# Dead products in the first stage's waits, two page gathers issued elsewhere, and strided copies turned round, in a TensorE-bound decoder layer

## Chip, cores and metric

One core of one Trainium2 chip. The metric is the device time of one execution in microseconds, as a median over runs. Lower is better.

## What is computed

One layer of a hybrid decoder over 512 prompt tokens and 32 sample tokens (8 sequences of 4), width 1024, all float32: a modulated RMS norm, then two mixers fed by one projection (sparse attention with a compressed, a selected and a window branch; a convolution module), merged by gates, one output projection, and a SwiGLU FFN of width 2816 with norms round it. Cut to what the change touches:

```python
ada = silu(c) @ w_ada + b_ada                     # six parts: shift, scale, gate, twice
h = rms_norm(x, g[0]) * (1 + sc_m) + sh_m
q, kv, g, glu, mg = split(h @ w_in)               # 16 heads, 4 kv heads, head width 64
conv_in = a * sigmoid(b)                          # a, b = split(glu), 512 channels
o_conv = silu(layer_norm(depthwise_conv31(hist))) @ w_pw2
# past keys and values: cache_kv[page_table], 4 pages of 128 rows for each of 8 sequences
k_c = gelu(flat(blocks of 32 rows) @ w_cmp1 + b_cmp1) @ w_cmp2     # and v_c
y = (ga * (gates of o_cmp, o_slc, o_win) + gb * o_conv) @ w_out
```

## The kernel before

**Products.** Nearly all the work is TensorE's. A float32 weight tile (`wraw`, 128 x 1024) is split into a high part (`wh`, ACT, L168) and a low part (`wl`, DVE, L171), the activations likewise (`hh`, `hl`). A half tile is 8 + 8 + 8 products of 128 x 272 (`hh·wh`, `hl·wh`, `hh·wl`), a tile two halves for the 544 tokens. All products but transposes go through one helper line, L165.

**Order.** Python code emits the program by events at hand-written times: `ev(t, f)` calls `f` at planner time `t`, `spawn` steps a generator whose `yield`s are times, `when(kind, n)` is the time of a weight. The weights come in the order of a plan, through rings of a few raw buffers (`wraw`, `araw`, `xraw`) loaded by SP's queue; a load starts when the buffer's last reader is done. A scheduler then orders each engine's rows by that order and by what it thinks is ready. Each engine works strictly in its order.

**First stage (0 to 69 us).** `x` is loaded, squared and summed; 18 + 21 `warm` products of a constant tile (`mm(dst, wt, src)`, result never read) run beside that. `rstd_from` turns the sums (products of 1 column). `conditioning(h)` makes half of the modulation vectors: eight `ada_product`s of raw weights with `cs` (32 columns, 256 wide), then `ada_quarters` (an eviction to `adaz`), `ada_first` (two transposes) and DVE work that ends with `A0`. `rows(k)` norms one of 8 row blocks, `opened(k)` makes the first three projection tiles (`w0h`, `w0l`) on it: blocks 0 to 3 after conditioning(0), 4 to 7 after conditioning(1).

**Pages.** The sample group's past comes as 32 pages, in four gathers `load_pages(bq)` of 8 indirect DMAs each on POOL's queue (L431). Gathers 0 and 2 share one buffer, 1 and 3 another, which later holds `Xc`. `paced(0, A0[:, 7, 8:9])` makes gather 0 wait, on POOL, for a one-element copy of `A0` of conditioning(1). `compress_pages(bq, kd)` are 16 products `pv<-X,w1t`, called pv(bq, kd) here.

**Convolution.** For each of four channel blocks POOL multiplies the sample windows (`cpr`, L638), DVE reduces them (L639), then 31 taps run on DVE, with the `wl` splits between. `compress_prompt` copies the prompt's keys and values (`zt`) into `Xc` on ACT (L762); near it ACT also evicts `K` (L719), and `qz` (L842), which `pt<-selq,qz` on TensorE needs.

**Attention and FFN.** Groups g = 0 to 3 with units i = 0 to 3: scores, exponentials `PB` on ACT, scaling on POOL and DVE, transposes (`big<-c,PB`, L1073) and value products, with the weight half tiles between. Then output projection, second norm and FFN.

Of the kernel before, what the change touches and what calls it, by code (L numbers as in the profile page):

```python
# [35 lines left out]
TP = 512  # L36
# [29 lines left out]
NF = 12  # L66
# [13 lines left out]
def _plan():  # L80

    p = [(0.1 * n, "ada", n) for n in range(8)] + [(1 + 0.1 * n, "glu", n) for n in range(NG)]
    p += [(2.345 + 0.1 * n, "ada", n) for n in range(8, 16)]
    p += [(43.845 + 6.5 * (n - NG), "glu", n) for n in range(NG, 8)]
    p += [(76.23 + 10.0 * n, "kv", n) for n in range(12)]
    p += [(60.955 + 5.024 * n, "ada", 16 + n) for n in range(16)]
    p += [(at(3, 1.759 + 0.428 * n), "ada", 32 + n) for n in range(16)]
    p += [(164, "g", 0)]
    p += [(205.59 + 3.412 * n, "pw2", n) for n in range(8)]
    p += [(111.427 + 9.999 * n, "qs", n) for n in range(8)]  # L90
    p += [(TA + 6.4 * n, "q", n) for n in range(2)]
    for g in range(4):
        if g < 3:
            p += [(at(g, 6.173 if g == 0 else 5.336), "q", 2 * g + 2), (at(g, 9.865) - 1.608, "q", 2 * g + 3)]
        p += [(at(g, 12.127 + 0.25 * n) if g < 3 else at(3, 0.321 + 0.9 * n), "ga", 2 * g + n) for n in range(2)]
# [17 lines left out]
def body(ctx, tc, xT, cT, cst, sel, vecs, b1row, wall, w1, pool_rows, kwin, vwin, convst, ptab,  # L113
# [356 lines left out]
    with tc.tile_pool(name="p0", bufs=1) as p0:  # L470
# [40 lines left out]
        def conditioning(h):  # L511
            p = P_pt()
            for k in range(8):
                raw, tag = take("ada", 8 * h + k)
                ada_product(p, k, raw)
                raw_done(tag)
            ada_first(h, ada_quarters(p))
            r = slice(4 * h, 4 * h + 4)
            first.append(dve.scalar_tensor_tensor(A0[:, r], adaT[:, 1, r], 1.0, gains[:, 0, r, None].to_broadcast([128, 4, 9]),
                                     op0=OP.add, op1=OP.mult))  # L520
# [109 lines left out]
    def conv(ct, t, step):  # L630

        y = cy[:, ct, :TP]
        ys = cy[:, ct, TP:].rearrange("p (b t) -> p b t", t=4)
        b = vc[:, V_BDW + ct:V_BDW + ct + 1]
        hs0 = hst[:, ct, :, 0:4]
        win = bass.AP(tensor=hs0.tensor, offset=hs0.offset, ap=[hs0.ap[0], [34, 8], [1, 4], [1, 31]])
        pr_ = cp.tile([128, 8, 4, 31], F32, name="cpr", tag="cpr", bufs=1)
        pool.tensor_mul(pr_, win, dw[:, ct, None, None, :].to_broadcast([128, 8, 4, 31]))  # L638
        dve.tensor_reduce(ys, pr_, axis=AX.X, op=OP.add)  # L639
        dve.tensor_scalar(ys, ys, b, None, op0=OP.add)  # L640
        for k in range(31):
            yield t + step * k
            w = dw[:, ct, k:k + 1]
            if k == 0:
                dve.tensor_scalar(y, hist[:, ct, 0:TP], w, b, op0=OP.mult, op1=OP.add)
            else:
                dve.scalar_tensor_tensor(y, hist[:, ct, k:k + TP], w, y, op0=OP.mult, op1=OP.add)  # L647

    def layer_norm(t):
# [99 lines left out]
    def compress_prompt(t):  # L749
        yield t - 12  # L750
        Xc = xp.tile([128, 2, 16, 64], F32, name="Xc", tag="X1")
# [3 lines left out]
        for kd in range(2):  # L755
            for pr in range(2):
                for h2 in range(2):
                    g = 2 * pr + h2
                    src = zts[kd, pr][64 * h2:64 * h2 + 64, 0:TP].rearrange("p (b l r) -> p r l b", b=16, r=2)
                    for r in range(2):  # L760
                        o = Xc[64 * r:64 * r + 64, kd, :, g * 16:g * 16 + 16]
                        act.activation(o, src[:, r], AF.Copy)  # L762
# [66 lines left out]
    def q_sample(f):  # L829
# [60 lines left out]
    spawn(99.808, compress_prompt(142.311))  # L890
    ada_b2 = []
# [127 lines left out]
    def unit(g, i, t, dq, dp):  # L1019
# [79 lines left out]
    def attn(g):  # L1099
        ev(at(g, 0) + 0.005, split_keys, g)  # L1100
        spawn(at(g, 0.15), compressed(g, at(g, 0.15)))
# [6 lines left out]

        ev(at(g, 0) + 6.411, units)

    def sample_attn(t0, step):
# [46 lines left out]
        yield t0 + 7.845  # L1158
        p = P_sc()
# [12 lines left out]
        for b in range(8):  # L1172
# [169 lines left out]
    def second_norm(hf, t, step):  # L1342
# [428 lines left out]
```

## Time and profile before

| | us |
|---|---|
| median of 3 runs (lowest to highest) | 1059.93 (1059.86 to 1061.65) |
| profiled execution | 1055.7 |
| its span in the trace | 1053.9 |
| TensorE busy | 1015.5 |

The profiled execution is 0.4% below the median, so a sum worked out from the trace is scaled by 1059.93/1055.7 before it is set against the median. The page's rows give for each group of instructions its busy time, and then the idle time of its engine just ahead of it with what ended that. TensorE's clock is given as a share of full speed: at 1.00 a 128 x 272 product takes 0.125 us of its queue, at 0.5 about 0.23.

### The profile page before, as it was taken

Reading aid. Unit: us, or ns where it says so; the run is one execution under the profiler, and the core shown is the slowest. Engines: PE = TensorE matmul, PEld = TensorE weight load, DVE = VectorE, ACT = ScalarE, POOL = GpSimd, SP = SyncE. Lnnn points to the kernel's source line nnn. Section 1 sums busy time; section 2 is a strip of 40 time slices with the busy share of each in tenths; the row PEclk is TensorE's granted clock in tenths of the full one; section 3 lists DMA queues with packets and bytes.
Section 4 is the critical chain, followed back from the end, with each engine's and each line's share of the span. In section 5 each row is a group of like instructions: output and inputs, shape, how many; then the busy total and the mean of one; then the engine's idle time right before and its main releaser. Section 6 shows DMA issues by size and latency. Waiting matters only on the chain.

```text
span 1053.9 us, 20870 instructions
## 1 busy us (share of the span) xinstructions
PE 1015.5 (96%) x8360; PEld 915.5 (87%) x8360; DVE 721.4 (68%) x1351; ACT 529.1 (50%) x1169; POOL 174.1 (17%) x175
## 2 busy tenths in 40 slices
PE   8789989999999999999999899999999999999996
PEld 7579889899986787787787599999999999999996
DVE  2469899334386676676766767899988888544644
ACT  3242212646455455654543556765666656444442
POOL 4064600000225253353421000000000000000000
PEclk8889989999999999999999999999999999999998
DMA  9854666332624424424434554555222232554652
GB/s 339 340 188 143 219 212 206 128 109 88 206 66 150 173 92 166 141 101 167 141 114 141 180 195 173 203 181 178 83 101 101 95 106 101 212 182 165 206 181 85
DMA packets 50001, 167.55 MB, mean 159 GB/s; under 512 B 6208, under 2 KB 8400, under 8 KB 49520
## 3 DMA queue, kind: packets, MB, share of 16 engines
q1 hardware_dynamic: 36432, 122.57, 33.9%
q0 software_dynamic: 6272, 22.42, 6.5%
q10 hardware_dynamic: 7200, 21.22, 5.4%
q8 instruction: 66, 1.08, 0.4%
q14 instruction: 31, 0.25, 0.1%
HBM read 149.38 MB, written 16.81 MB: 158 GB/s over the span
## 4 chain that ended last, share of the span: by engine, by line
PE 86%; DMA 6%; DVE 3%; ACT 2%; POOL 1%; issue 1%; SPq 0%; DVEq 0%; ACTq 0%
PE mm L165 52%; PE pv L165 12%; PE big L165 11%; PE pt L165 5%; PE big L1073 4%; DMA wraw<-in_wall_dram 2%; DMA araw<-in_wall_dram 2%; POOL X L431 1%; ACT Xc L762 1%; DMA x<-in_xT_dram 1%; DVE wl L171 1%; DMA X<-in_rows_dram,idx 1%; ACT PB L1045 1%; DMA vw<-in_vwin_dram 0%; PE big L1201 0%
## 5 line engine op out<-in xcount | busy, mean ns | idle before, releaser
L168 ACT ACTIVATE wh<-wraw 128x1024 fp32r<-128x1024 f32 (+1 forms) x183 | 165.9, 908 | 168.9 <-PE mm L165 99.1
L171 DVE TENSOR_TENSOR wl<-wraw,wh 128x1024 fp32r<-128x1024 f32 (+1 forms) x135 | 156.6, 1160 | 127.2 <-ACT wh L168 114.7
L165 PE MATMUL mm<-hh,wh 128*128 128x272 f32 (+1 forms) x608 | 174.8, 313 | 4.6 <-ACT zt L729 4.6
L165 PE MATMUL mm<-hl,wh 128*128 128x272 f32 (+1 forms) x608 | 172.0, 309 | 0.0
L165 PEld LDWEIGHTS mm<-hh,wh 128*128 128x128 f32 x608 | 118.5, 195 | 15.5 <-issue 5.5
L165 PEld LDWEIGHTS mm<-hl,wh 128*128 128x128 f32 x608 | 118.1, 194 | 7.3 <-issue 4.4
L165 PE MATMUL mm<-hh,wl 128*128 128x272 f32 (+1 forms) x608 | 100.1, 303 | 0.0
L165 PEld LDWEIGHTS mm<-hh,wl 128*128 128x128 f32 x608 | 85.8, 190 | 5.6 <-issue 2.3
L165 PE MATMUL mm<-uh,wh 128*128 128x272 f32 x352 | 90.2, 289 | 0.2 <-ACT wh L168 0.2
L165 PE MATMUL mm<-ul,wh 128*128 128x272 f32 x352 | 90.1, 288 | 0.0
L1045 ACT ACTIVATE PB<-big,mx 128x128 f32<-128x128 f32 (+3 forms) x128 | 65.9, 526 | 47.5 <-DVE mx L1042 37.0
L647 DVE SCALAR_TENSOR_TENSOR cy<-hist,vc,cy 128x512 f32<-128x512 f32 x120 | 83.2, 747 | 0.5
L165 PE MATMUL mm<-h2h,wh 128*128 128x272 f32 x328 | 77.3, 288 | 0.0
L1053 POOL TENSOR_SCALAR PB<-PB,mx 128x128 f32<-128x128 f32 (+3 forms) x56 | 59.2, 1073 | 82.6 <-DVE mx L1050 55.7
L165 PE MATMUL mm<-h2l,wh 128*128 128x272 f32 x260 | 66.8, 287 | 0.0
L165 PEld LDWEIGHTS mm<-uh,wh 128*128 128x128 f32 x352 | 66.4, 189 | 0.4 <-ACT wh L168 0.4
L165 PEld LDWEIGHTS mm<-ul,wh 128*128 128x128 f32 x352 | 66.2, 188 | 0.0
L165 PEld LDWEIGHTS mm<-h2h,wh 128*128 128x128 f32 x328 | 58.4, 188 | 0.0
L165 PE MATMUL mm<-h2h,wl 128*128 128x272 f32 x312 | 53.0, 288 | 0.5 <-ACT pv L1540 0.5
L165 PE MATMUL mm<-uh,wl 128*128 128x272 f32 x352 | 52.2, 288 | 0.0
L1042 DVE TENSOR_REDUCE mx<-big 128x2 f32<-128x256 f32 (+3 forms) x64 | 50.5, 816 | 0.2
L165 PEld LDWEIGHTS mm<-h2l,wh 128*128 128x128 f32 x260 | 48.9, 188 | 0.0
(471 smaller groups left out, 2259.5 us busy)
## 6 DMA issues: line engine op xcount, KB each, us to landing
wraw<-in_wall_dram SPq DMA_DIRECT2D x174, 512.0 KB, 4.1
araw<-in_wall_dram SPq DMA_DIRECT2D x12, 512.0 KB, 8.5
wraw<-in_wall_dram SPq DMA_DIRECT2D x16, 384.0 KB, 3.5
xraw<-in_wall_dram SPq DMA_DIRECT2D x8, 512.0 KB, 5.5
kw<-in_kwin_dram ACTq DMA_DIRECT2D x8, 512.0 KB, 3.5
out_wk_dram<-kw ACTq DMA_DIRECT2D x8, 512.0 KB, 5.2
vw<-in_vwin_dram ACTq DMA_DIRECT2D x8, 512.0 KB, 3.5
out_wv_dram<-vw ACTq DMA_DIRECT2D x8, 512.0 KB, 2.6
```

What stands on the lines that cost most here:

```text
L165: pe.matmul(out, lhsT, rhs, start=start, stop=stop, **more)
L168: act.activation(dst, src, AF.Copy, scale=scale)
L171: (eng or dve).tensor_sub(dst, src, h.bitcast(F32))
L431: pool.indirect_dma_start(out=X[:, pg], out_offset=None, in_=rows2, in_offset=bass.IndirectOffsetOnAxis(ap=idx[:, 0, col:col + 1], axis=0))
L647: dve.scalar_tensor_tensor(y, hist[:, ct, k:k + TP], w, y, op0=OP.mult, op1=OP.add)
L762: act.activation(o, src[:, r], AF.Copy)
L1042: dve.tensor_reduce(mx[:, 0, r, 2 * jj:2 * jj + 2], sc[:, :, :w], axis=AX.X, op=OP.max, negate=True)
L1045: act.activation(P[r][:, :, j * 128:j * 128 + 128], sc[:, jp, :w].rearrange("p (k n) -> p k n", n=128), AF.Exp, bias=mx[:, 0, r, j:j + 1], ...
L1053: (dve if r or g == 3 and i > 1 else pool).tensor_scalar(v, v, m[:, j:j + 1], None, op0=OP.mult)
L1073: pe.transpose(p[:, x, j * 128:j * 128 + 128], P[r][:, kt, j * 128:j * 128 + 128], ident)
```

## The change

Five edits, in the words of the diff. `warm` products are added round the ada products of conditioning(0) and behind both conditionings (`z` is `adaz`; their bank is `pw`, or a `P_pv` bank in conditioning(1)). Gather 0 is paced by the raw weights of conditioning(1)'s seventh ada product in place of `A0`. Gather 2 is issued behind the fourth `cpr`, in place of an event of its own. The `Xc` copies go through their 256 elements with `b` innermost, in place of `l`. Some thirty planner times change.

```diff
             for k in range(8):
                 raw, tag = take("ada", 8 * h + k)
                 ada_product(p, k, raw)
+                if h and k == 6:
+                    paced(0, raw[:, 0:1])
+                if h == 0 and 0 < k < 7:
+                    warm(3, raw[:, 0:128])
                 raw_done(tag)
-            ada_first(h, ada_quarters(p))
+            z = ada_quarters(p)
+            wb = pw if h == 0 else P_pv()
+            warm(3, raw[:, 0:128], wb[:, 0:128])
+            ada_first(h, z)
+            warm(7, z[:, 0:128], wb[:, 0:128])
...
         rstd_from([acc, last], (rs[:, :HT], rs[:, HT:]), 1024, (P_mm, P_mm))
+        warm(9, wt)
         conditioning(0)
...
                 conditioning(1)
-                paced(0, A0[:, 7, 8:9])
...
-        pool.tensor_mul(pr_, win, dw[:, ct, None, None, :].to_broadcast([128, 8, 4, 31]))
+        ins = pool.tensor_mul(pr_, win, dw[:, ct, None, None, :].to_broadcast([128, 8, 4, 31])).ins
+        if ct == 3:
+            with tc.issue_after(ins):
+                load_pages(2)
...
-    ev(XT + 16, load_pages, 2)
...
-                    src = zts[kd, pr][64 * h2:64 * h2 + 64, 0:TP].rearrange("p (b l r) -> p r l b", b=16, r=2)
+                    src = zts[kd, pr][64 * h2:64 * h2 + 64, 0:TP].rearrange("p (b l r) -> p r b l", b=16, r=2)
                     for r in range(2):
-                        o = Xc[64 * r:64 * r + 64, kd, :, g * 16:g * 16 + 16]
+                        o = Xc[64 * r:64 * r + 64, kd, :, g * 16:g * 16 + 16].rearrange("p l b -> p b l")
                         act.activation(o, src[:, r], AF.Copy)
...
-        spawn(t, conv(ct, max(t, 40.379 + 29.131 * ct), 0.659))
+        spawn(t, conv(ct, max(t, 40.379 + 29.131 * ct), 1.196))
...
-                yield t + 18.289 + (bq + 0.402 * kd) * step
+                yield t + 16.198 + (bq + 0.451 * kd) * step
...
-        ev(when("qs", f) + 3.18, rest)
+        ev(when("qs", f) + 1.981, rest)
...
-            yield t + dq + (b + 0.162) * dp / nb
+            yield t + dq + (b + 0.121) * dp / nb
...
-        ev(at(g, 0) + 6.411, units)
+        ev(at(g, 0) + 5.914, units)
```

The other times that change: the plan's times of some weights, steps of `zhalf`, `pw2`, the conv norm, the second norm, the sample attention, loads of `x`, and the last norm, mostly by 0.01 to 3.

TensorE, conditioning(1)'s end and the first products of rows k = 4, before (`big` and `mm` are banks of the opened tiles, `pv` that of the pages):

```order
L165 MATMUL pt<-wraw,cs 32x256 x4
L325 MATMUL pt<-c,adaz 128x128 x2
L165 MATMUL mm<-hh,w0h 128x272
L165 MATMUL big<-hh,w0h 128x272 x2
L165 MATMUL mm<-hh,w0l 128x272
L165 MATMUL mm<-hl,w0h 128x272
```

The same place now:

```order
L165 MATMUL pv<-wraw,hl 128x128 x3
L325 MATMUL pt<-c,adaz 128x128 x2
L165 MATMUL pv<-adaz,hl 128x128 x7
L165 MATMUL mm<-hh,w0h 128x272
L165 MATMUL big<-hh,w0h 128x272 x2
L165 MATMUL mm<-hh,w0l 128x272
L165 MATMUL mm<-hl,w0h 128x272
L165 MATMUL mm<-hh,w0h 128x272
L165 MATMUL mm<-hh,w0l 128x272
L165 MATMUL pv<-X,w1t 128x128
L165 MATMUL mm<-hh,w0h 128x272
```

The first product of gather 0's pages stood behind all rows of k = 4 to 7; now it stands behind seven products of k = 4, and ten dead products stand round the transposes.

POOL's queue, the four `cpr` and gathers 2 and 3 (X rows; 8 to a gather), before:

```order
L638 TENSOR_TENSOR cpr<-hst,vc 128x992
L753 DMA b_1692<-in_b1row_dram 1x16x16
L798 DMA selt<-in_sel_dram 48x256
L638 TENSOR_TENSOR cpr<-hst,vc 128x992
L431 DMA X<-in_rows_dram,idx 128x512 x6
L638 TENSOR_TENSOR cpr<-hst,vc 128x992
L431 DMA X<-in_rows_dram,idx 128x512 x9
L638 TENSOR_TENSOR cpr<-hst,vc 128x992
L431 DMA X<-in_rows_dram,idx 128x512
```

And now:

```order
L646 TENSOR_TENSOR cpr<-hst,vc 128x992
L764 DMA b_1734<-in_b1row_dram 1x16x16
L809 DMA selt<-in_sel_dram 48x256
L646 TENSOR_TENSOR cpr<-hst,vc 128x992 x2
L431 DMA X<-in_rows_dram,idx 128x512 x6
L646 TENSOR_TENSOR cpr<-hst,vc 128x992
L431 DMA X<-in_rows_dram,idx 128x512 x10
```

The third `cpr` moved ahead of the gathers. The six that stand between it and the fourth are now of gather 3; gather 2's eight stand behind the fourth, with the last two of gather 3.

ACT, the `Xc` copies, before:

```order
L762 ACTIVATE Xc<-zt 64x16x16 x9
L719 ACTIVATE K<-mm 128x272
L762 ACTIVATE Xc<-zt 64x16x16 x3
L842 ACTIVATE qz<-pt 128x128
L762 ACTIVATE Xc<-zt 64x16x16 x4
```

And now:

```order
L773 ACTIVATE Xc<-zt 64x16x16 x9
L730 ACTIVATE K<-mm 128x272
L773 ACTIVATE Xc<-zt 64x16x16 x7
L733 DMA out_kv_dram<-K 128x544
L853 ACTIVATE qz<-pt 128x128
```

`qz` stood behind twelve copies and stands behind all sixteen; on TensorE the product that reads it moved behind a whole half tile.

More of the change, by code (lines that the diff above doesn't have):

```diff
@@ L85, in _plan @@
     p += [(76.23 + 10.0 * n, "kv", n) for n in range(12)]
-    p += [(60.955 + 5.024 * n, "ada", 16 + n) for n in range(16)]
+    p += [(60.955 + 4.999 * n, "ada", 16 + n) for n in range(16)]
     p += [(at(3, 1.759 + 0.428 * n), "ada", 32 + n) for n in range(16)]
     p += [(164, "g", 0)]
-    p += [(205.59 + 3.412 * n, "pw2", n) for n in range(8)]
-    p += [(111.427 + 9.999 * n, "qs", n) for n in range(8)]
-    p += [(TA + 6.4 * n, "q", n) for n in range(2)]
+    p += [(205.225 + 3.412 * n, "pw2", n) for n in range(8)]
+    p += [(114.6 + 9.999 * n, "qs", n) for n in range(8)]
+    p += [(TA + 6.539 * n, "q", n) for n in range(2)]
     for g in range(4):
@@ L94, in _plan @@
             p += [(at(g, 6.173 if g == 0 else 5.336), "q", 2 * g + 2), (at(g, 9.865) - 1.608, "q", 2 * g + 3)]
-        p += [(at(g, 12.127 + 0.25 * n) if g < 3 else at(3, 0.321 + 0.9 * n), "ga", 2 * g + n) for n in range(2)]
+        p += [(at(g, 12.146 + 0.25 * n) if g < 3 else at(3, 0.308 + 0.9 * n), "ga", 2 * g + n) for n in range(2)]
     for n, (g, x) in enumerate(((0, 1.6), (0, 3.4), (0, 4.8), (0, 8.0), (1, 4.5), (1, 7.7), (2, 4.5), (2, 7.7))):
@@ L99, in _plan @@
     p += [(TO + 31.9 + 3 * n, "out1", n) for n in range(5)]
-    p += [(TO + 50.55 + 3 * NF * hf + 3 * n, "fi%d" % hf, n) for hf in range(2) for n in range(NF)]
+    p += [(TO + 50.137 + 3 * NF * hf + 3 * n, "fi%d" % hf, n) for hf in range(2) for n in range(NF)]
     p += [(TS + 0.01 * n, "sf", n) for n in range(NF, 44)]
-    p += [(TG + 66 * hf + 7.662 * ft + 3.064 * kg, "fo%d" % hf, fo_entry(ft, kg))
+    p += [(TG + 64.062 * hf + 7.662 * ft + 3.13 * kg, "fo%d" % hf, fo_entry(ft, kg))
           for hf in range(2) for ft in range(8) for kg in range(3)]
@@ L299, in first @@
             zhalf(kind, w, 0, rh, rl, nk, evac)
-            ev(t + 0.349 * nk, zhalf, kind, w, 1, rh, rl, nk, evac)
+            ev(t + 0.367 * nk, zhalf, kind, w, 1, rh, rl, nk, evac)
         ev(t, first)
@@ L675, in layer_norm @@
         rstd_from([acc], rs, 512, (P_sc, P_sc))
-        yield t + 19.079
+        yield t + 21.589
         cyh = cp.tile([128, 4, T], F32R, name="cyh", tag="hist")
@@ L693, in compress_sample @@
             for kd in range(2):
-                yield t + 18.289 + (bq + 0.402 * kd) * step
+                yield t + 16.198 + (bq + 0.451 * kd) * step
                 compress_pages(bq, kd)
-        yield t + 18.187 + 3.6 * step
+        yield t + 19.365 + 3.6 * step
         p = P_sc()
@@ L749, in compress_prompt @@
     def compress_prompt(t):
-        yield t - 12
+        yield t - 11.733
         Xc = xp.tile([128, 2, 16, 64], F32, name="Xc", tag="X1")
@@ L871, in first @@
             zhalf("pw2", w, 0, cyhl[0], cyhl[1], 4, ev_p)
-            ev(t + -1.758, zhalf, "pw2", w, 1, cyhl[0], cyhl[1], 4, ev_p)
+            ev(t + -2.016, zhalf, "pw2", w, 1, cyhl[0], cyhl[1], 4, ev_p)
         ev(t, first)
@@ L889, in body @@
             n += 1
-    spawn(99.808, compress_prompt(142.311))
+    spawn(99.888, compress_prompt(141.835))
     ada_b2 = []
@@ L1099, in attn @@
     def attn(g):
-        ev(at(g, 0) + 0.005, split_keys, g)
+        ev(at(g, 0.173) + -0.36, split_keys, g)
         spawn(at(g, 0.15), compressed(g, at(g, 0.15)))
@@ L1149, in sample_attn @@
         dve.tensor_mul(pcp[:, :, 0:16], s, m_[:, :, None].to_broadcast([128, 4, 16]))
-        yield t0 + 0.372
+        yield t0 + 3.145
         p = P_pt()
@@ L1157, in sample_attn @@
             act.activation(PCT[a, bh], p[a, 0:128], AF.Copy)
-        yield t0 + 7.845
+        yield t0 + 7.795
         p = P_sc()
@@ L1197, in sample_attn @@
             dve.tensor_scalar(pr_[:, :544], pr_[:, :544], mx[:, 1:2], None, op0=OP.mult)
-            yield t + 0.222 * step
+            yield t + 0.236 * step
             p = P_big()
@@ L1322, in body @@
     for k in range(0, 8, 2):
-        ev(TO + 7.86 + 1.706 * k, load_x, k)
+        ev(TO + 5.248 + 1.706 * k, load_x, k)
     A2 = yp.tile([128, 8, 9], F32, name="A2")
@@ L1355, in second_norm @@
                     dve.tensor_add(acc2, acc2, sq)
-        yield t + 4 + 7.475 * step
+        yield t + 3.696 + 7.475 * step
         rs = rstd_from([acc2, sq], None, 1024, (P_pv,))
         for k in range(8):
-            yield t + 8.497 + (8.399 + k) * step
+            yield t + 4.975 + (8.233 + k) * step
             norm_rows(yp, k, hf, x1[:, k], rs, A2, adaT[:, 3], h2h, h2l)
@@ L1391, in body @@
     for n, ft in enumerate(KEPT + (0, 1, 2, 3, 4)):
-        ev(TO + 26.151 + 3 * n if n < 3 else when("out1", ft), out_tile, 1, ft, n == 0, n == 7)
-    spawn(TO + 24.2, second_norm(0, TO + 24.715, 0.806))
-    spawn(TO + 47.393, second_norm(1, TO + 49.67, 1.1))
+        ev(TO + 26.151 + 2.961 * n if n < 3 else when("out1", ft), out_tile, 1, ft, n == 0, n == 7)
+    spawn(TO + 24.407, second_norm(0, TO + 24.715, 0.806))
+    spawn(TO + 47.393, second_norm(1, TO + 49.67, 1.875))
     run_until(TO + 48.1)
@@ L1609, in body @@
     spawn(TG + 64.115, last_norm(0, TG + 66.2, 1.0))
-    spawn(TG + 133, last_norm(1, TG + 133, -0.168))
+    spawn(TG + 133, last_norm(1, TG + 133.609, -0.168))
     run()
```

## Prediction

> **What bounds the kernel now.** I read the page first, then TensorE's waits, then a table of time windows with the granted clock, and at last the engines' timelines round each wait. From the page, the busy time and the chain that ended last:
>
> ```profile
> PE 1015.5 (96%) x8360; PEld 915.5 (87%) x8360; DVE 721.4 (68%) x1351; ACT 529.1 (50%) x1169; POOL 174.1 (17%) x175
> PE 86%; DMA 6%; DVE 3%; ACT 2%; POOL 1%; issue 1%; SPq 0%; DVEq 0%; ACTq 0%
> ```
>
> TensorE (PE) works 1015.5 of 1053.9 us, so only its 38.4 idle us and its slow stretches can be won. Who it waits for, longest total first:
>
> ```profile
> PE mm L165 <- ACT zt L729: 4.6, 2, 2.8
> PE mm L165 <- ACT hh L407: 3.5, 2, 1.8
> PE pv L165 <- DMA X<-in_rows_dram,idx: 3.1, 1, 3.1
> PE pt L165 <- ACT qz L842: 2.3, 1, 2.3
> PE big L1073 <- ACT PB L1045: 2.0, 2, 1.2
> ```
>
> Columns of the windows: window, length, busy time (instructions) of PE, PEld, DVE, ACT, POOL, then PE clock, DMA share, GB/s.
>
> ```profile
> 25.20:32.00 6.80, 3.11 (x38) 0.79 (x30) 1.00 (x5) 1.44 (x2) 0.00 (x0) 0.99 1.03 413
> 32.00:42.30 10.30, 8.36 (x35) 6.50 (x35) 9.98 (x21) 5.89 (x11) 0.00 (x0) 0.51 1.01 373
> 42.30:48.20 5.90, 5.90 (x51) 5.75 (x54) 0.00 (x0) 0.00 (x0) 0.00 (x0) 1.00 0.79 321
> 52.30:54.00 1.70, 0.02 (x1) 0.00 (x0) 1.57 (x7) 0.54 (x2) 0.90 (x2) 1.00 0.77 255
> 56.00:59.40 3.40, 3.40 (x16) 3.40 (x16) 3.40 (x10) 2.78 (x6) 2.79 (x3) 0.50 0.65 221
> 69.60:73.10 3.50, 3.50 (x18) 3.50 (x18) 0.75 (x1) 0.00 (x0) 1.87 (x2) 0.51 0.70 118
> 127.00:130.00 3.00, 1.23 (x11) 1.01 (x9) 0.00 (x0) 1.34 (x2) 2.90 (x2) 1.00 0.98 339
> 130.00:135.00 5.00, 5.00 (x32) 4.76 (x36) 4.79 (x7) 0.40 (x1) 2.57 (x4) 0.66 1.00 369
> 142.00:145.00 3.00, 3.00 (x15) 3.00 (x16) 3.00 (x5) 0.40 (x1) 0.00 (x0) 0.54 0.27 101
> 196.00:199.20 3.20, 0.85 (x8) 0.71 (x7) 0.69 (x1) 3.10 (x7) 0.00 (x0) 1.00 0.36 128
> 199.20:202.70 3.50, 3.50 (x17) 3.50 (x18) 0.00 (x0) 3.43 (x7) 0.00 (x0) 0.52 0.20 80
> ```
>
> The pattern to see: each stretch in which PE was idle for half or more is followed by one of 3.4 us or more at half clock (0.50 to 0.54, or 0.66 over a 5 us window). So a wait is paid twice: its own length, and 3.4/2 = 1.7 us behind it. That holds for the waits at 53, 66, 128, 140 and 197 us. The change touches all five.
>
> **A: first stage, extra products and gather 0.** PE and POOL in order of time, with the idle time before an instruction and its releaser in brackets:
>
> ```profile
> 1.38 5.91 PE L165 MATMUL big<-hl 128*128 128x128 f32 x36 [1.38 <-DVE hl L488]
> 54.03 0.39 PE L165 MATMUL mm<-hh,w0h 128*128 128x272 f32 x1 [1.72 <-ACT hh L407]
> 55.81 0.45 PE L165 MATMUL mm<-hh,w0h 128*128 128x272 f32 x1 [0.26 <-ACT hh L168]
> 68.86 0.94 PE L165 MATMUL pv<-X,w1t 128*128 128x128 f32 x6 [3.15 <-DMA X<-in_rows_dram,idx]
> 52.95 0.19 POOL L541 COPY pace<-A 128x1 f32<-128x1 f32 x1 [34.38 <-DVE A L519]
> 53.29 0.98 POOL L431 DMA_INDIRECT X<-in_rows_dram,idx  x1
> 63.42 0.95 POOL L431 DMA_INDIRECT X<-in_rows_dram,idx  x1 [0.31 <-issue]
> ```
>
> The change adds 9 + 18 + 3 + 7 dead products in conditioning(0) and 3 + 7 in conditioning(1). The first row gives their price: 36 records are 18 calls in 5.91 us from a cold start, 0.33 us a call; at twice the clock about half, 0.16, which I round up to 0.22. Thirty calls behind the rstd products cost 4.8 to 10 us of PE, against 3.7 us of idle in 25.2 to 32.0 and a cold wait at 31 to 33. But rows k = 0 to 3 are held by DVE there (9.98 of 10.3 us), not by PE. So I bound the delay of conditioning(1) by −0.7 (clock held from 32 us) and +1.0, and take +0.5. The 7 calls behind the transposes of conditioning(1) fill the 1.72 us at 53: the half clock of 56.0 to 59.4 goes, −1.7.
>
> Gather 0 now follows a copy of the raw weights of the seventh ada product. That load sits behind a DMA that is full until 42 us; it should land at 42 to 44. The eight gathers take 63.42 − 53.29 = 10.1 us to issue, and PE got the last page 68.86 − 63.42 = 5.4 us later. So the pages land at 57.5 to 59.5 instead of 68.86; I take 58. The order puts the first page product far ahead, which is the price of the early gather: PE is strictly in order and everything behind it stands. It comes after the seventh product of rows k = 4, at 55.8 + 0.5 = 56.3. Stall 1.7 us, then the other row products, 65.7 − 55.8 − 1.7 = 8.2 us at full clock: end at 66.2 (65.7 is where PE's wait of 3.15 before 68.86 begins). Before, the like point is 68.86 plus the 1.7 of half clock behind it, 70.56. So −4.4; if the new stall brings its own half clock, −2.7. I take −3.7. Ends: pages at 55.5, −6.0; last page 10 us after issue, at 64.4, with half clock, +3.7.
>
> **B: gather 2 and the third and fourth cpr.**
>
> ```profile
> 101.76 2.17 POOL L638 TENSOR_TENSOR cpr<-hst,vc 128x992 f32<-128x992 f32 x1
> 127.08 0.94 POOL L431 DMA_INDIRECT X<-in_rows_dram,idx  x1 [0.30 <-issue]
> 128.04 2.14 POOL L638 TENSOR_TENSOR cpr<-hst,vc 128x992 f32<-128x992 f32 x1
> 103.97 1.19 DVE L639 TENSOR_REDUCE cy<-cpr 128x32 f32<-128x992 f32 x1 [2.38 <-POOL cpr L638]
> 121.73 1.23 DVE L171 TENSOR_TENSOR wl<-wraw,wh 128x1024 fp32r<-128x1024 f32 x1
> 130.21 1.19 DVE L639 TENSOR_REDUCE cy<-cpr 128x32 f32<-128x992 f32 x1 [4.84 <-POOL cpr L638]
> 128.56 1.06 ACT L168 ACTIVATE wh<-wraw 128x1024 fp32r<-128x1024 f32 x1 [7.12 <-DMA wraw<-in_wall_dram]
> 140.38 1.06 ACT L168 ACTIVATE wh<-wraw 128x1024 fp32r<-128x1024 f32 x1 [9.66 <-DMA wraw<-in_wall_dram]
> 153.61 2.62 PE L165 MATMUL pv<-X,w1t 128*128 128x128 f32 x22
> ```
>
> A chain of five queues: POOL computes cpr behind page gathers, DVE waits for it, the split wl behind that on DVE frees a raw weight buffer late, the next weight load starts late, ACT's wh waits for it, and the zt eviction behind wh holds PE's bank. After the change the third cpr stands ahead of all gathers: DVE's 2.38 us go, the wl of 121.73 comes at about 119.3, its load lands some 2.4 us earlier than 128.56, and the first PE gap (3.0 − 1.23 = 1.77 us) with its half clock goes: −3.5. The fourth cpr stands behind six gathers instead of seven: one gather with its pause is 128.04 − 127.08 + 0.30 = 1.3 us, so the second gap (2.78) shrinks by 1.3 and may keep its half clock. Sum −4.8. Ends: −1.3 if the first load stays late for another reason, −8.0 if both gaps go with both half clocks. Gather 2 itself loses cover. Its eight now follow the fourth cpr, at about 122 to 126 in the old time, take 10.1 us to issue and 5.4 to land: 138 to 142. PE wants them at 153.61 less a half tile (3.0), less what A and B save (8.5): 142.1. I count no stall, but by a hair.
>
> **C: compressed copies.** The group of the copies, their place on ACT, PE's wait behind them, and an ACT group of like length that reads and writes in order:
>
> ```profile
> L762 ACT ACTIVATE Xc<-zt 64x256 f32<-64x256 f32 x16 | 10.4, 649 | 0.2
> 190.53 6.00 ACT L762 ACTIVATE Xc<-zt 64x256 f32<-64x256 f32 x9
> 196.43 0.37 ACT L719 ACTIVATE K<-mm 128x272 f32<-128x272 f32 x1
> 198.77 0.28 ACT L842 ACTIVATE qz<-pt 128x128 f32<-128x128 f32 x1
> 199.10 0.42 PE L165 MATMUL pt<-selq,qz 128*128 128x32 f32 x2 [2.35 <-ACT qz L842]
> L996 ACT ACTIVATE sn<-sn 128x256 f32<-128x256 f32 x4 | 1.7, 417 | 4.9 <-DVE sn L995 4.9
> ```
>
> Today each copy reads with a stride of 128 bytes and writes in a row: 649 ns against 417. The change reads every 8 bytes and writes every 256. No row shows a scattered write, so the price lies between 0.42 (only reads cost) and 0.65 (writes cost as much), or above at 0.9 (both). I take 0.42, since the read pattern is the one known to differ from the fast rows. Then all sixteen copies and the K eviction end at 190.53 + 16 × 0.42 + 0.37 = 197.6 and qz at 197.9. Its product on PE is set behind a half tile of 24 products (3.0 us) and comes at 199.10 − 2.35 + 3.0 = 199.75: no wait. The 2.35 us ahead of 199.10 and the 1.7 of half clock go, −4.0. At 0.65 qz ends at 201.6 and PE stands 1.85: −0.5. At 0.9 it stands 5.9: +3.5.
>
> [...]
>
> **D: the other order numbers.** In attention some transposes move about 20 products ahead, but those belong to the last unit of the group before, whose exponentials are long done; PE's waits for PB are 2.0 us in all. The rest shifts by a half tile. ±1, and I take +1.0 for waits that 60 moved places may open. Sum: −3.7 − 4.8 − 4.0 + 1.0 = −11.5 against the profiled execution (1055.7 us, 0.4% below the median of 1059.93); on the median 1048.4.
>
> **Rivals.** (1) Slower, one mechanism: gather 0 lands in a full DMA. From pages at 60.7 the first stage loses, since 60.7 + 8.2 + 1.7 is 70.6. Together with B and C at their small ends (−1.3, −0.5) it makes the whole slower by 0.2% (2.1 us, about what can be told from no change) only if the pages land after 64.5 us; at 65, with D at nothing, 1062.5. For it: the DMA share is 1.01 until 42.3 us, where the gathers would begin. Against: it falls to 0.79 behind. (2) The dead products do not hold the clock and only delay: A −1.0, total about 1051. (3) The copies stay at 0.65: 1052. (4) The pages of gather 2 come late at pv(2,0) and PE stands 3 us there with a half clock: B +0, total 1053. (5) The three gains miss together ((2), (3) and (4)): −1.0 + 0 − 0.5 + 1.0, 1059.4, no change.
>
> **Numbers.** Chances: forecast 0.42, (2) 0.12, (3) 0.20, (4) 0.10, (1) 0.08, (5) 0.08. All of the first four are faster by over 0.2%; (5) is the same; (1) is slower. The range goes from −16.5 (A and B near their good ends) to rival 4 with more lost, 1043.5 to 1057.5; that leaves out (1), (5) and a little below.
>
> **What would show it.** Right: clock 1.00 at 56 to 59 and at 70 to 73; first X product of PE at 56 to 60; no PE wait for DMA X above 2 us; DVE's reduce of the third cpr without a wait; copies near 0.42 us; no wait for qz. Wrong: a wait of over 4 us at the first X product, Xc copies at 0.65 or above, a wait at pv(2,0), or a group of new PB waits between 300 and 600 us.

## The result, and the profile after

| | us |
|---|---|
| before, median in this comparison | 1059.93 |
| after, median of 5 runs (lowest to highest) | 1054.99 (1053.54 to 1056.19) |
| ratio, with its 95% interval | 0.9949 [0.9935, 0.9964] |
| profiled execution after (its span) | 1054.71 (1052.9) |
| forecast (range) | 1048.4 (1043.5 to 1057.5) |

Faster, inside the range, but by 4.9 us where 11.5 were forecast. A second comparison of the same changed kernel over 12 runs (e5 below) gave 0.9986 [0.9976, 0.9995]. The intervals do not meet, so the gain is told as 1.5 to 5 us. Single executions of either kernel spread over 5 to 8 us: before lies between 1055.7 and 1063.3 in the runs here, after between 1053.5 and 1059.1. The profiled executions of before (1055.7) and of e5 (1053.71, where its median is 1057.40) were among the fastest of their kernels. So no term is settled below by the two first traces alone. One of e9's twelve executions took 3418.31 us and is left out of its ratio.

From the page of after, busy time and chain:

```profile
PE 1015.9 (96%) x8454; PEld 918.6 (87%) x8454; DVE 726.8 (69%) x1351; ACT 529.5 (50%) x1169; POOL 169.3 (16%) x175
PE 78%; DVE 10%; DMA 6%; ACT 3%; issue 2%; POOL 1%; SPq 0%; ACTq 0%; DVEq 0%
```

PE is busy as long as before (1015.5), with 94 records more. DVE's share of the chain rose from 3% to 10%, its busy time by 5.4 us at the same 1351 instructions: the same work takes DVE longer. PE's longest waits after:

```profile
PE pt L165 <- ACT qz L853: 4.7, 1, 4.7
PE mm L165 <- ACT zt L740: 3.5, 2, 2.9
PE pv L165 <- DMA X<-in_rows_dram,idx: 2.9, 1, 2.9
PE mm L165 <- ACT wh L168: 2.1, 2, 1.4
```

The wait for `qz` doubled (2.3 before), those for `zt` shrank from 4.6 to 3.5, and the one for the pages is still 2.9. The windows that answer to those of before, same columns:

```profile
25.20:32.00 6.80, 6.80 (x68) 4.78 (x69) 0.67 (x4) 1.33 (x2) 0.00 (x0) 1.00 1.03 410
52.30:54.00 1.70, 1.70 (x16) 1.59 (x14) 1.38 (x6) 0.35 (x1) 0.00 (x0) 1.00 0.90 265
56.00:59.40 3.40, 0.73 (x3) 0.76 (x4) 3.40 (x11) 2.71 (x5) 0.00 (x0) 0.89 0.47 190
60.00:62.00 2.00, 2.00 (x11) 2.00 (x11) 2.00 (x4) 0.70 (x2) 0.00 (x0) 0.50 0.14 27
69.60:73.10 3.50, 3.50 (x30) 3.50 (x30) 1.74 (x5) 2.95 (x6) 3.50 (x4) 1.00 0.82 223
130.00:135.00 5.00, 5.00 (x38) 4.41 (x36) 5.00 (x8) 0.20 (x1) 4.30 (x3) 0.66 0.90 274
142.00:145.00 3.00, 2.09 (x24) 1.03 (x24) 3.00 (x6) 0.40 (x1) 0.12 (x1) 1.00 1.03 417
201.80:205.30 3.50, 3.50 (x16) 3.50 (x17) 1.22 (x1) 1.65 (x4) 0.00 (x0) 0.53 0.06 11
```

The half clock at 69.6 and 142 is gone. That at 130 (0.66) and behind `qz` (0.53) stands. At 56 to 59.4, where PE ran at half clock before, it now mostly stands (0.73 of 3.40 us busy), and a half clock follows that wait at the pages (0.50 at 60 to 62).

To see where the time went, three points that stand behind the same products in both orders but for the 47 dead ones: pv(0,1), the first product of `spr` in attention, the last norm's `rsT`. PE's timeline, before and then after:

```profile
89.10 3.73 PE L165 MATMUL pv<-X,w1t 128*128 128x128 f32 x32
320.12 0.77 PE L1201 MATMUL big<-c,spr 128*128 128x128 f32 x5 [0.73 <-ACT PB L1045]
1044.49 0.91 PE L165 MATMUL pt<-c,rsT 96*128 96x96 f32 x6 [0.56 <-DVE rsT L386]
```

```profile
87.13 3.73 PE L165 MATMUL pv<-X,w1t 128*128 128x128 f32 x32
320.07 0.77 PE L1211 MATMUL big<-c,spr 128*128 128x128 f32 x5 [1.23 <-ACT PB L1055]
1043.49 0.91 PE L165 MATMUL pt<-c,rsT 96*128 96x96 f32 x6 [0.56 <-DVE rsT L386]
```

The same for one more execution of each (e1 and e5), with differences of the means. The first column holds A, the second B and C, the third D. With two executions of each kernel, these differences are rough:

| | pv(0,1) at | from there to `spr` | from there to the last `rsT` |
|---|---|---|---|
| before; e1 | 89.10; 90.17 | 231.02; 233.51 | 724.37; 725.28 |
| after; e5 | 87.13; 89.61 | 232.94; 228.91 | 723.42; 723.94 |
| after − before | −1.3 | −1.3 | −1.1 |
| forecast | −3.7 | −8.8 | +1.0 |

### The profile page after: what moved, and what is told of

Same layout as the page of the kernel before. It is cut to its first block, busy times and chain, and to the rows that moved or that the text cites. A ratio compares the mean times of both kernels' runs of the same rounds, so it can differ in the third digit from the quotient of the medians.

```text
span 1052.9 us, 21049 instructions
## 1 busy us (share of the span) xinstructions
PE 1015.9 (96%) x8454; PEld 918.6 (87%) x8454; DVE 726.8 (69%) x1351; ACT 529.5 (50%) x1169; POOL 169.3 (16%) x175
## 4 chain that ended last, share of the span: by engine, by line
PE 78%; DVE 10%; DMA 6%; ACT 3%; issue 2%; POOL 1%; SPq 0%; ACTq 0%; DVEq 0%
PE mm L165 48%; PE big L165 10%; PE pv L165 9%; DVE cy L658 6%; PE pt L165 5%; PE big L1083 4%; DMA wraw<-in_wall_dram 3%; DMA araw<-in_wall_dram 1%; DVE wl L171 1%; ACT Xc L773 1%; DMA X<-in_rows_dram,idx 1%; DMA x<-in_xT_dram 1%; ACT PB L1055 1%; POOL X L431 1%; DMA vw<-in_vwin_dram 1%
## 5 line engine op out<-in xcount | busy, mean ns | idle before, releaser
L165 PE MATMUL mm<-hl,wh 128*128 128x272 f32 (+1 forms) x608 | 168.3, 304 | 0.0
L165 PEld LDWEIGHTS mm<-hh,wh 128*128 128x128 f32 x608 | 116.7, 192 | 16.5 <-issue 6.4
L658 DVE SCALAR_TENSOR_TENSOR cy<-hist,vc,cy 128x512 f32<-128x512 f32 x120 | 88.0, 789 | 0.4
L165 PEld LDWEIGHTS mm<-ul,wh 128*128 128x128 f32 x352 | 66.2, 188 | 0.0
L165 PEld LDWEIGHTS mm<-h2h,wh 128*128 128x128 f32 x328 | 58.5, 188 | 0.0
```

The lines of the kernel that those rows point to most:

```text
L165: pe.matmul(out, lhsT, rhs, start=start, stop=stop, **more)
```

## Experiments

Theory: the change is worth what its parts do where they meet a wait. The dead products delay as much as they gain by the clock; the reordered copies are as slow as the old ones; the moved gather 2 wins nothing. Rival: every part gains about as forecast, and something else, the new planner times above all, takes it back. All kernels compute the whole layer. Each ratio is to before in runs on the same chip.

| | what it is | median us | ratio | interval |
|---|---|---|---|---|
| e1 | before, word for word | 1059.45 | 1.0005 | [0.9992, 1.0018] |
| e2 | before + first-stage edits | 1058.56 | 0.9990 | [0.9970, 1.0011] |
| e9 | before + dead products alone | 1062.13 | 1.0023 | [1.0008, 1.0038] |
| e11 | before + all edits, planner times of before | 1057.75 | 0.9999 | [0.9981, 1.0017] |
| e5 | after, word for word | 1057.40 | 0.9986 | [0.9976, 0.9995] |
| e3 | after, copies in the old order | 1057.91 | 0.9986 | [0.9971, 1.0001] |
| e4 | after, copies that write in a row | 1052.28 | 0.9935 | [0.9914, 0.9956] |
| e6 | after, first page product behind the rows | 1055.54 | 0.9977 | [0.9963, 0.9990] |
| e7 | after, gather 2 at its old event | 1054.23 | 0.9964 | [0.9950, 0.9977] |
| e8 | e4 and e6 | 1052.32 | 0.9935 | [0.9921, 0.9950] |
| e10 | after, without the dead products ahead of and between the ada products | 1052.65 | 0.9938 | [0.9921, 0.9956] |
| e12 | e4, e6, e7 and e10 | 1043.36 | 0.9851 | [0.9830, 0.9873] |

**e1, e5: both kernels again.** No edit.

> The kernel before, word for word, to see how far two executions of one program differ. Theory 1 (the gain on the median was larger than the two traces show because the trace of before is a lucky execution, 4.2 us under its median): ratio 1.000 within 0.002, and a trace whose span lies 3 to 6 us over 1053.9, with the surplus in waits or half-clock stretches ahead of 260 us. Theory 2 (something lies outside the span): the same span, 1053 to 1055, with a time of 1059 to 1061.

> The changed kernel, word for word, beside its variants on one chip. In the second run's three kernels with this first stage, ACT's rsT (L385) came at 19.3 to 19.8 us, 3.8 us after the sums it reads, and at 15.5 in the first trace. Theory 1 (this is chance from execution to execution): again 0.995 of before within 0.002, and a trace with rsT at either time. Theory 2 (it is the kernel's own and the first trace an exception): rsT at 19 to 20, ratio 0.997 or more.

They give the spread told above. e1's profiled execution took 1060.18 us, 4.5 more than that of before, with 4.57 us of wait at the second `zt` in place of 2.85.

**e2, e9: the first stage alone.** e2 adds to before the dead products and the new point of gather 0; e9 the dead products only. e9 against e2:

```diff
-                if h and k == 6:
-                    paced(0, raw[:, 0:1])
...
+                paced(0, A0[:, 7, 8:9])
```

> The kernel before with only the dead products and the new point of gather 0. Theory 1 (the first stage carries the whole gain of the change, the rest cancels): 4 to 5 us faster than before, ratio about 0.9955. Theory 2 (the stall at the early page product eats it): 2 us faster or less, ratio 0.998 to 1.000; the first X product waits 2 to 4 us with a half clock behind it in both.

> The kernel before with only the dead products; gather 0 waits for A0 as before. In five executions with these products the end of conditioning(1) came at 56 to 61 us, against 51.9 and 52.6 before, and the DMA share fell to about 0.6 at 25 to 30 us. Theory 1 (the dead products, with the rstd products now ahead of the first ada products, hold the raw buffers longer, the weight loads start later and conditioning(1) waits for its weights): conditioning(1) ends at 56 to 60, DMA share 0.5 to 0.7 at 25 to 30, 2 to 4 us slower than before (ratio 1.002 to 1.004). Theory 2 (gather 0 in the middle of the loads delays them): conditioning(1) ends at 52 to 53, faster than before by 2 us for the clock.

The dead products alone, with the order that comes with them, cost 2.4 us (0.23%). In the trace they delay conditioning(1), and the pages, still paced by `A0`, with it. PE of e9:

```profile
54.20 0.38 PE L325 MATMUL pt<-c,adaz 128*128 128x128 f32 x2
72.33 1.62 PE L165 MATMUL pv<-X,w1t 128*128 128x128 f32 x6 [5.88 <-DMA X<-in_rows_dram,idx]
```

The transposes that end conditioning(1) came at 51.88 before. With the early gather as well, e2 ends where before does (within its interval).

**e10: fewer dead products, and the old order.** It keeps the dead products round the transposes of the two conditionings. With the other 27 gone, the first ada product stands ahead of the rstd products again, as before the change; so e10 takes back two things at once:

```diff
-                if h == 0 and 0 < k < 7:
-                    warm(3, raw[:, 0:128])
...
-        warm(9, wt)
```

> The changed kernel without the nine dead products ahead of conditioning(0) and without the three behind each of its products; those round the transposes of both conditionings stay, and the first ada products stand ahead of the rstd products again. Theory 1 of the run before: conditioning(1) ends at 52 to 53.5, DMA share 1.0 until 45, and 2 to 4 us faster than the changed kernel on this chip, ratio to before 0.994 to 0.996. Theory 2: conditioning(1) still ends at 56 or later, ratio as the changed kernel's, 0.9986.

0.9938. Windows from 25 to 30 us of before, after, e5 and e10 in this order, columns as above:

```profile
25.00:30.00 5.00, 2.87 (x40) 0.77 (x32) 0.00 (x0) 0.06 (x1) 0.00 (x0) 0.97 1.02 407
```

```profile
25.00:30.00 5.00, 4.90 (x51) 2.87 (x51) 0.00 (x0) 0.00 (x0) 0.00 (x0) 1.00 1.03 410
```

```profile
25.00:30.00 5.00, 5.00 (x59) 2.91 (x51) 0.00 (x0) 0.00 (x0) 0.00 (x0) 1.00 0.78 269
```

```profile
25.00:30.00 5.00, 3.13 (x32) 0.72 (x32) 0.00 (x0) 0.00 (x0) 0.00 (x0) 0.72 1.03 410
```

Before and in e10 the DMA is full (1.02, 1.03) and PE has room. In the first trace of after, with the same dead products as e5, the DMA is full too (1.03). Of these four, only e5 has a full PE and a DMA that is not full (0.78). Of e5, the start of `rsT` on ACT, on PE the first ada product and the end of conditioning(1), and on SP's queue the load that waits for a free buffer:

```profile
19.45 0.26 ACT L385 ACTIVATE rsT<-mm,epst 96x6 f32<-96x6 f32 x1 [6.18 <-remote]
...
24.68 0.64 PE L165 MATMUL pt<-wraw,cs 128*32 128x256 f32 x8
...
57.71 0.63 PE L165 MATMUL pt<-wraw,cs 128*32 128x256 f32 x3 [0.80 <-issue]
59.03 0.38 PE L325 MATMUL pt<-c,adaz 128*128 128x128 f32 x2
...
12.12 14.85 SPq L236 DMA_DIRECT2D araw<-in_wall_dram  x2
```

The same of after:

```profile
15.47 0.26 ACT L385 ACTIVATE rsT<-mm,epst 96x6 f32<-96x6 f32 x1 [2.43 <-PE mm L165]
...
18.66 0.64 PE L165 MATMUL pt<-wraw,cs 128*32 128x256 f32 x8
...
52.13 0.38 PE L325 MATMUL pt<-c,adaz 128*128 128x128 f32 x2
...
11.91 9.04 SPq L236 DMA_DIRECT2D araw<-in_wall_dram  x2
```

The change put the rstd products, which need `rsT`, ahead of the first ada product, so all that follows on PE waits for `rsT`. PE has made the sums that `rsT` reads by 15.7 in e5 and 15.4 in after, where ACT starts at once; in e5 it starts 3.8 us later. The first ada product then comes at 24.68 in place of 18.66, and the waiting load gets its buffer at 26.97 in place of 20.95 (24.31 before). From there PE cannot catch up: in e5 an ada product and its three dead ones take 1.43 us, while the DMA at 410 GB/s would bring a weight tile of 512 KB in 1.28 us (an estimate from these rows). All traces, by the start of `rsT`:

| | `rsT` starts | DMA share, 25 to 30 us | conditioning(1) ends |
|---|---|---|---|
| ada product first, no dead products among them: before, e1, e10, e12 | 16.9 to 19.1 | 1.02 to 1.03 | 51.9 to 52.6 |
| rstd products first, all dead products: after, e9, e11 | 15.5 to 16.0 | 1.02 to 1.03 | 52.1 to 54.2 |
| the same: e6, e7, e8 | 16.5 to 17.9 | 1.01 to 1.02 | 56.4 to 58.5 |
| the same: e2, e3, e4, e5 | 19.3 to 19.8 | 0.54 to 0.78 | 59.0 to 61.5 |

So the delay goes with a late `rsT`, and only in the new order. How much of it the order would cost without the dead products, these runs do not separate, since e10 and e12 take both back. In e6 to e8 conditioning(1) is late although that window is full, so the window is not the whole account. Nor does the trace of e10 show its 0.5% in the first stage: pv(0,1) stands at 89.03 there (89.61 in e5), for PE waits 4.41 us for the early page, with a half clock behind it.

**e6: the first page product held.** In after PE stands 2.92 us at a page ahead of the row products. e6 puts pv(0,0) behind the last row product:

```diff
     def compress_pages(bq, kd):
...
-        for l in range(16):
+        with tc.issue_after(end[0]):
+            for l in range(16):
...
-                        mm(gl[f][hf][:, :HT], w[:, k], r[:, k, sl], k == 0 and part == 0, k == 7 and part == 2)
+                        end[:] = [pe.matmul(gl[f][hf][:, :HT], w[:, k], r[:, k, sl], start=k == 0 and part == 0,
+                                            stop=k == 7 and part == 2).ins]
```

> The changed kernel with pv(0,0)'s products held on TensorE behind the last product of the rows k = 4 to 7; nothing else is asked of the order. Theory 1 (the early page product costs the stall and its half clock): no DMA X wait, rows end at 64 to 65 where rsT is early, 4 us faster than the changed kernel (ratio to before about 0.991); where rsT is late, the pages are there anyway and it makes no difference (0.995). Theory 2 (what is won is given back at the next weight load): a new wait on wraw or wh between 65 and 130 of the same size, 0.995.

0.9977 against e5's 0.9986: no wait for `X` is left, but the gain is not settled from none. In e5 conditioning(1) was so late that the pages (PE at 62.66) were waited for by nobody. The hold has something to win only where conditioning(1) is on time, as in after and in e10, whose PE stands:

```profile
59.97 0.76 PE L165 MATMUL pv<-X,w1t 128*128 128x128 f32 x2 [4.41 <-DMA X<-in_rows_dram,idx]
```

There the rows end at 70.55; in e12, which adds the hold, at 64.37.

**e7: gather 2 back at its event.**

```diff
-        if ct == 3:
-            with tc.issue_after(ins):
-                load_pages(2)
...
+    ev(XT + 16, load_pages, 2)
```

> The changed kernel with gather 2 issued by its old event ahead of the convolution. Theory 1 (the new point of gather 2 gains by freeing the fourth cpr): the wait at 139 to 143 is 2.5 to 4.5 us again with a half clock behind it, 3 to 5 us slower than the changed kernel (ratio 0.998 to 1.000). Theory 2 (the waits at 128 and 140 come from the splits' order, not from cpr): same as the changed kernel within 1 us.

0.9964: undoing this part made the kernel no slower; the ratio is 0.2% under e5's, with intervals that just touch. Taps and `cpr` tell why moving the third `cpr` won so little. The 120 taps as a group (min, median, max ns), before and after:

```profile
L647 DVE SCALAR_TENSOR_TENSOR cy<-hist,vc,cy x120: 733/747/757, 69.6 to 188.2; 128x512 f32<-128x512 f32 x120
```

```profile
L658 DVE SCALAR_TENSOR_TENSOR cy<-hist,vc,cy x120: 731/742/2655, 72.7 to 188.0; 128x512 f32<-128x512 f32 x120
```

And POOL's third `cpr` after, DVE beside it, the `wl` behind, and ACT's `wh`:

```profile
100.03 2.56 POOL L646 TENSOR_TENSOR cpr<-hst,vc 128x992 f32<-128x992 f32 x1 [13.72 <-issue]
```

```profile
99.82 3.32 DVE L658 SCALAR_TENSOR_TENSOR cy<-hist,vc,cy 128x512 f32<-128x512 f32 x2
...
121.91 1.21 DVE L171 TENSOR_TENSOR wl<-wraw,wh 128x1024 fp32r<-128x1024 f32 x1
```

```profile
128.02 1.06 ACT L168 ACTIVATE wh<-wraw 128x1024 fp32r<-128x1024 f32 x1 [8.55 <-DMA wraw<-in_wall_dram]
```

Before, DVE stood idle 2.38 us while POOL made the product. Now it has work, but the tap that meets the `cpr` takes up to 2.66 us in place of 0.74: two taps in 3.32 us. From the second reduce to the third DVE took 17.34 us before and 16.14 after, with one tap (0.67) fewer: of the idle 2.38 us it won about 0.5, and the rest became a stretched tap. The new order then sets the `hist` and `hst` rows, 0.42 us, ahead of this `wl`, so `wl` and `wh` come when they came before (121.73 and 128.56).

**e3, e4: the copies.** e3 is after with the copies of before. e4 turns the tile round, so that a copy reads every 8 bytes and writes in a row:

```diff
-        Xc = xp.tile([128, 2, 16, 64], F32, name="Xc", tag="X1")
+        Xc = xp.tile([128, 2, 64, 16], F32, name="Xc", tag="X1")
...
-                        o = Xc[64 * r:64 * r + 64, kd, :, g * 16:g * 16 + 16].rearrange("p l b -> p b l")
+                        o = Xc[64 * r:64 * r + 64, kd, g * 16:g * 16 + 16]
...
-                mm(p[64 * kd:64 * kd + 64, 0:128], Xc[:, kd, l], w1t[kd][:, l], l == 0, False)
+                mm(p[64 * kd:64 * kd + 64, 0:128], Xc[:, kd, :, l], w1t[kd][:, l], l == 0, False)
```

> The changed kernel with the compressed copies reading and writing in the old order; every engine's order of instructions stays. Theory 1 (a scattered write costs as much as a scattered read): copies 0.64 to 0.65 us, the qz wait 4.5 to 4.9 us, time within 1 us of the changed kernel (ratio to before about 0.995). Theory 2 (the new order is cheaper at least for some): copies 0.66 or more, 1 us or more slower than the changed kernel.

> The changed kernel with Xc laid out so that a copy reads every 8 bytes and writes 16 elements in a row; the products then read Xc as stationary operand with a stride of 64 bytes. Theory 1 (the 256-byte write step costs what the 128-byte read step did): copies about 0.42 us, qz wait 1.0 to 1.4 us instead of 4.7, its half clock gone, 4 to 5 us faster than the changed kernel (ratio to before about 0.990), unless the 32 products on Xc get slower. Theory 2 (the price is in the 16 x 16 pattern or in 64 partitions, not in the lines): copies stay at 0.64 and the time within 1 us of the changed kernel.

The copies (min, median, max ns) after, in e3 and in e4, and PE's weight loads of `Xc` after and in e4:

```profile
L165 PEld LDWEIGHTS pt<-w1t,Xc x64: 133/137/137, 225.1 to 228.4; 128*64 128x64 f32 x64
...
L773 ACT ACTIVATE Xc<-zt x16: 627/638/671, 190.7 to 200.8; 64x256 f32<-64x256 f32 x16
```

```profile
L773 ACT ACTIVATE Xc<-zt x16: 627/640/676, 192.7 to 202.9; 64x256 f32<-64x256 f32 x16
```

```profile
L165 PEld LDWEIGHTS pt<-w1t,Xc x64: 186/206/230, 221.4 to 225.1; 128*64 128x64 f32 x64
...
L773 ACT ACTIVATE Xc<-zt x16: 426/432/452, 191.2 to 198.1; 64x256 f32<-64x256 f32 x16
```

Turning the scatter from reads to writes changed nothing: 638 against 640 ns. Without a scatter, still at 16 x 16 elements in 64 partitions, it is 432, so e4's second theory falls; by "the lines" it means how far apart in memory the neighbouring elements of a copy lie. The scatter then sits in PE's weight loads, 206 against 137 ns, nearly hidden beside the products: the 64 product records of `Xc` take 3.8 us from the first start to the last in place of 3.5. ACT's `qz`, and PE at the product that reads it, in after, and the latter in e4:

```profile
201.42 0.28 ACT L853 ACTIVATE qz<-pt 128x128 f32<-128x128 f32 x1
```

```profile
201.75 0.42 PE L165 MATMUL pt<-selq,qz 128*128 128x32 f32 x2 [4.66 <-ACT qz L853]
```

```profile
198.90 0.41 PE L165 MATMUL pt<-selq,qz 128*128 128x32 f32 x2 [0.48 <-ACT qz L853]
```

**e8: e4 and e6.**

> The changed kernel with pv(0,0) held as in the second run of this set and with the Xc copies written in rows. Theory 1 (the two gains add): 0.989 or less of before. Theory 2 (the first stage's part is chance): 0.9935, as with the row copies alone.

0.9935, as e4 alone: beside row copies the hold gained nothing that these runs can tell.

**e11: all edits with the planner times of before.**

> The change's edits to dead products, both gathers and the copies with all planner times of before. Theory 1 (the planner times carry part of the gain, in the FFN's norms above all): 1 to 3 us slower than the changed kernel, ratio 1.000 or more. Theory 2 (they do nothing in sum): 0.9986 like the changed kernel.

0.9999 against e5's 0.9986; the intervals overlap. The rival falls: the new times do not eat a gain of the size forecast. If anything they bring 1.4 us, and the edits without them bring nothing that can be told.

**e12: what pays, together.** The edits of e4, e6, e7 and e10 on after: tail dead products, early gather 0 with pv(0,0) held, gather 2 at its event, row copies, new planner times.

> The changed kernel with the parts that looked good put together: dead products only round the transposes, pv(0,0) held behind the rows, gather 2 at its old event, Xc copies written in rows. Theory 1 (the gains add): 0.989 to 0.991 of before. Theory 2 (each takes away what the other wins): 0.9935 like the row copies alone.

1043.36 us, 0.9851 [0.9830, 0.9873], faster than both kernels. Against e5 the four edits alone gave (each by its ratio to before on its own chip) −0.48% (e10), −0.51% (e4), −0.22% (e7) and −0.09% (e6), in sum −1.30%; e12 gave −1.35%. The sum is that neat only against e5: against the first comparison (0.9949) the four give +0.18% in sum, and e12 −0.98%. PE at the end of the first stage, and two windows there:

```profile
64.37 0.83 PE L165 MATMUL pv<-X,w1t 128*128 128x128 f32 x6
```

```profile
56.00:59.40 3.40, 3.25 (x26) 3.25 (x26) 3.40 (x10) 2.66 (x6) 0.00 (x0) 1.00 0.45 174
60.00:65.00 5.00, 5.00 (x43) 5.00 (x41) 2.78 (x5) 1.23 (x5) 0.35 (x1) 1.00 0.47 145
```

The rows end at 64.37 at full clock, no wait for a page; pv(0,1) starts at 83.1 against 89.10. So A's gain, forecast −3.7 with −6.0 as the good end, was there to be had, with fewer dead products and the page product held. Against the mean of after and e5, e12's trace is 5.3 us ahead at pv(0,1) and wins 7.3 more up to `spr`.

## Why the prediction was wrong in size

The sign and the range were right. Every gaining term was too large:

- **A, −3.7 forecast, −1.3 in the table, and nothing over more traces.** Seven traces hold all of A without the hold (after, e2, e3, e4, e5, e7, e11): pv(0,1) stands at 87.1 to 92.0 in them, 89.6 in the mean, as in the two of before. What was right: the pages (58 forecast, 58.67 in the first trace), the wait of 1.72 at 53 filled, the half clock at 69.6 to 73.1 gone. The failed step is "I bound the delay of conditioning(1) by −0.7 (clock held from 32 us) and +1.0". In the first trace it holds (52.13 for 51.88); in the nine other traces with all dead products (e2 to e9, e11) conditioning(1) ended 1.9 to 9.6 us late, and e10, without 27 of the 47 and with the old order, put it back to 51.95. I priced the products against PE's idle time in 25 to 32 us, and left out that the 18 between the ada products each hold a weight buffer that a load is waiting for, so that a PE that comes late stays late (1.43 us a step in e5). I also saw that the edit moves the rstd products ahead of the ada products, which makes PE wait for `rsT`, and put that at nothing without a reason. A smaller miss: the stall at the page was 2.92, not 1.7, with a half clock behind it (0.50 at 60 to 62), so the rows ended at 68.65 in place of 66.2.
- **B, −4.8 forecast, about nothing from the gather.** The failed step is "DVE's 2.38 us go, the wl of 121.73 comes at about 119.3"; it came at 121.91, and the first PE gap, which was to go, grew from 1.77 to 2.91 us (2.72 in e5). An idle time on DVE was taken for time that work could fill. All but 0.5 us of it could not be, since beside POOL's `cpr` a tap took up to 2.66 us in place of 0.74. The two taps and the `cpr` between 99.82 and 103.14 took 3.32 us together, where one after the other they would take about 3.5 (2 x 0.67 + 2.17, an estimate from the rows of before). These runs show that the two hold each other up, not why; I had not reckoned with it. The second gap did shrink (2.85 to 0.58) and lost its half clock, but in e7, with gather 2 put back, it is 1.51 against 1.43 in e5, and the clock is 1.00 behind it too, so the gather did not do it. In its place came small waits of 0.91 (`xraw`) and 1.39 us (`wh`). That gather 2 arrives without a stall was right.
- **C, −4.0 forecast, a small loss.** The failed step is "I take 0.42". The copies took 0.638, as rival 3 has it. A scattered write cost what a scattered read did: 638 ns with writes 256 bytes apart (after), 640 with reads 128 bytes apart (e3), 432 with reads 8 bytes apart and writes in a row (e4). My price for that case, PE standing 1.85 us, was short as well: it stood 4.66 (3.26 in e5). `qz` came at 201.42, as reckoned (201.6), but PE came to its product at 197.1 and not at 199.75: I had left PE's arrival where it was, though A and B were to bring PE forward and the copies, which start at 190.67 (190.53 before), did not move with it. From the last `h1v` products (at 194.75 before and 191.34 after) to `spr` the time grew by 3.4 us in the first pair of traces, 1.0 of it eight products of 0.125 us that moved behind that point; between e1 and e5 it grew by 0.6. e4 is the forecast come true: copies of 432 ns, a wait of 0.48, and 0.5% less time.
- **D, +1.0 forecast, −1.1 measured.** The same stretch spreads from 723.2 to 726.9 us over the traces with the new order numbers, so D is about nothing. The wait of 0.46 for `ya` at 634.9 is gone, and PE's waits for `PB` in the units are 2.1 us as before (2.0); only the one at `spr` grew, from 0.73 to 1.23 (0.68 in e5).
- **The half clock, 1.7 us in each of A, B and C.** "So a wait is paid twice" held for every wait of 1.5 us or more in the trace of before. Over the thirteen other traces it is a chance: of 32 waits of PE of 1.5 us or more between 60 and 206 us, 18 were followed within 5 us by a stretch at half clock, all six above 3.6 us and 12 of the 26 shorter ones. The same wait at 128 us was followed by 0.50 in after (2.91 us) and by 1.00 in e5 (2.72 us).

B and C together make −1.3 in the table, from values that differ by 4 us between two executions of the same kernel; what part of it is the order numbers, these runs do not settle. Of the rivals, (3) came about, and (2) in its second half: the dead products did hold the clock (1.00 at 25 to 30 in after and e5, 0.97 before), but in most traces they and the order mainly delay. The chain in (1) did not: the pages landed at 58.67. That the time fell inside the range is in part luck: A, B and C all missed, as in rival (5), which the range left out, and at e5's ratio the time would have been 1058.4, outside it.

Open stays why ACT starts `rsT` at 15.5 in some executions and up to 4 us after its sums in others, with an idle time that the profile of e5 puts down to "remote". In before it starts at 19.14, just as the sums, made at half clock (0.50 at 17 to 19 us), are done (19.1), and the first ada product stands ahead of the products that read it.

## What to carry to other kernels

Ask of a dead product that is to keep the clock up whether a load is waiting for the buffers that the products behind it release: in e5, where TensorE had come late, a stretch bound by the DMA became one bound by TensorE (from 25 to 30 us TensorE busy 5.00 of 5.00 us at a DMA share of 0.78, against 2.87 at 1.02 before). A look at the order that an edit makes is worth as much as a price for its instructions: here it put a wait for another engine ahead of the products that release the buffers. A half clock behind a short wait was a chance here and not a fixed price (12 of 26 waits of 1.5 to 3.6 us). Before an idle engine's time is booked as a gain, ask whether the work that would fill it can run beside what it waits for (here a tap took up to 2.66 us in place of 0.74). A transposing copy cost the same here whichever side was scattered (638 ns with scattered writes, 640 with scattered reads, 432 with neither); give the tile the writer's order, and let the scatter fall on a reader that is nearly hidden (here 64 weight loads of 206 ns in place of 137, some 0.3 us in all).

## What the runs showed of the hardware that I had not expected

- A DVE tap of 128 x 512 with two tensor inputs took 0.74 us (median of 120 in after) and up to 2.66 us while POOL multiplied 128 x 992. POOL's product, 2.13 to 2.17 us in three of four cases before and 2.61 in the other, took 2.56 to 3.02 in after.
- ACT's copy of 64 x 256 float32 took 638 ns with writes scattered at 256 bytes (after), 640 with reads at 128 bytes (e3), 432 with reads 8 bytes apart and writes in a row (e4).
- A weight load on TensorE whose columns lie 64 bytes apart took 206 ns in e4, in place of 137 in after; beside the products the 64 of them cost some 0.3 us in all (3.8 us for 3.5).
- A PE wait of 1.5 to 3.6 us was followed by a stretch at half clock in some executions and not in others (12 of 26, in thirteen traces).
